# A two-layer diffusion transformer: head outputs summed ungated, the first gate's sums off TensorE, softmax inverses through DRAM, later weight fetches

## The chip, the cores and the metric

The kernel runs on 1 core of one Trainium2 chip. The metric is the device time of one execution in microseconds (us): the median of 3 runs was 1186.27 us before the change (1185.79 to 1186.78). A difference in it under about 2 us is small beside everything that the kernel does: some 5,500 matrix products and 193 MB of transfers.

The engines are named as the profile names them: PE is TensorE's matmul, PEld its weight load, DVE VectorE, ACT ScalarE, POOL GpSimd, and SP the engine that issues most transfers.

## The reference

Two layers over 256 image tokens (x) and 256 context tokens (ctx), D = 1024. Layer 0 mixes tokens by retention (4 heads, values of 512), layer 1 by attention to a neighbourhood of 8 x 16 grid positions plus the context (32 heads of 32). Each layer ends with a squared-relu MLP of 4096. Shift, scale and gate of every part come from a conditioning vector c (c_ctx for the context).

```python
mod = (silu_c @ ada_w[i] + ada_b[i])[:, None, :]
sh1, sc1, g1, sh2, sc2, g2 = jnp.split(mod, 6, axis=-1)
h = x * (1.0 + sc1) + sh1
y, yc = retention_mixer(h, hc, ...)  if i % 2 == 0 else  neighbourhood_mixer(h, hc, ...)
x = layer_norm(DN_ALPHA * x + g1 * y, ln_g[i, 0], ln_b[i, 0])
h = x * (1.0 + sc2) + sh2
x = layer_norm(DN_ALPHA * x + g2 * sq_relu_mlp(h, mlp_w1[i], mlp_w2[i]), ln_g[i, 1], ln_b[i, 1])
# the context goes the same way in layer 0, with its own modulation
# retention:  y = concat over heads( norm(o) * silu(g) ) @ w_o
# neighbourhood:  prob = softmax(concat(q.k + bias, q.k_ctx));  o = prob @ (v, v_ctx)
```

## The kernel before, in words

**Products.** Each f32 product is three products of a high and a low part (`mm3`: hi·hi, hi·lo, lo·hi). A weight unit is a 512 KB block: SP fetches it into one of four `raw` buffers, ACT casts the high part (`hi`), DVE subtracts to get the low part (`lo`). `fetch` issues the transfer and the cast, `lows` the subtraction, `take` hands out units and runs five ahead.

**Order.** A framework puts the instructions of each engine into their final order. Where a line sets `.on` for an engine, its instructions stay in the order written.

**Layer 0.** Eight chunks of 128 columns first (`chunk_*`): each chunk's shift and scale are made on PE, its input is transposed (`chunk_turn`) and modulated, and head 0's Q and V begin. `turn_over` puts filler products on PE ahead of chunk 0. Then come heads 0 to 3. A head has the projections of Q, K and V (Q and V of head 0 fall into the chunks), the rotation on DVE (t, qkh, qkl), gates (pg), scores (pS), the value products (po), and the output projection (pw), each of whose 128x512 results is multiplied by the first gate g1 on DVE (`gated`) and added on POOL to the residual R (`accumulate`). R was scaled by ALPHA on ACT in head 0, so R collects ALPHA·x + g1·y. The last head adds on DVE and is followed by layer norm and the MLP.

**Background stream.** The other modulations are made step by step between the heads' products by `bg()`: each step loads one 512 KB block of `ada_w` and uses the one loaded a step earlier. A part has eight steps. `bg_max` bounds the steps, `bg_until` forces them. The first gate, part (0, 0, 2), runs on PE in head 0 (`ada_mm`: four narrow products a step, into pada); `first_gate` loads it as soon as it is there, since head 0's output needs it. The parts (0, 1, ...) for the MLP of layer 0 are weighted sums on DVE (`weigh`, four 128x512 instructions a step, in spare space named strips). Layer 1's parts are the same in 128x1024 (two instructions a step, acc), and run in layer 0's MLP.

**Layer 1.** The neighbourhood attention takes 16 steps n (8 groups of four heads, two query tiles). The table `STEPS` says for each which weight units are fetched ahead of its scores and softmax (`early`), which behind (`late`), and which projections (K, Q, V) stand between. `scores` writes pqk on PE; `soften` takes the biased minimum on DVE and the exponential with its sum on ACT; `flip` transposes the exponentials (ppt to pt); `attend` multiplies with the values (pav, rows natv) and scales by the inverse sums. For that scaling, `invert` takes the reciprocal of the sums (128x4), DVE spreads it to 128x128 (rr), `flip_sums` transposes it on PE, and `turned` copies it to rt on ACT. V(0) to V(3) are the value projections of the second half of the heads (pnv); the first of them, in the sixth step (n = 5), is the first to use their four weight units.

Of the kernel before, what the change touches and what calls it, by code (L numbers as in the profile page):

```python
# [104 lines left out]
def kernel(  # L105
# [324 lines left out]
    def ada_bias(l, offs, nb):  # L430
        brow = scr("brow")
        ab = ada_b[l]
        for i in range(2):
            sp.dma_start(
                out=brow[64 * i : 64 * i + 64, :nb],
                in_=bass.AP(ab.tensor, ab.offset + offs[i], [[nb, 2], [0, 32], [1, nb]]),
            )
        return brow

    def ada_mm(pr, k, nb, rhs):  # L440

        lhsT = cT[:, k, :, :].rearrange("p a t -> p (a t)")
        for j in range(4):
            pe.matmul(
                pr[32 * j : 32 * j + 32, 0:nb],
                lhsT=lhsT,
                rhs=rhs(j),
                start=(k == 0),
                stop=(k == KC - 1),
                tile_position=(0, 32 * j),  # L450
            )

    def ada_row(pr, brow, nb, p0=0, p1=P, row=None):
        if row is None:
            row = smp.tile([P, 256], F32, tag="row", name=nm("row"), bufs=1)
        dve.tensor_add(out=row[p0:p1, :nb], in0=pr[p0:p1, 0:nb], in1=brow[p0:p1, :nb])
        return row

# [76 lines left out]
    def bg_stream():  # L535
# [3 lines left out]
        for l, w, part in (  # L539
            [(0, 0, 2), (0, 1, 0), (0, 1, 1), (0, 1, 2)]  # L540
            + [(1, 0, 0), (1, 0, 1), (1, 0, 2), (1, 1, 0), (1, 1, 1), (1, 1, 2)]
        ):
            sh, sc, g = 3 * w * D, (3 * w + 1) * D, (3 * w + 2) * D
            offs = (sh + 512 * part, sc + 512 * part) if part < 2 else (g, g + 512)
            for n in range(KC):
                plan.append((l, w, part, offs, n))
        nxt = bg_load(*plan[0])
        yield
        for step, (l, w, part, offs, n) in enumerate(plan):
# [5 lines left out]
            if on_pe(l, w, part):  # L555
                if n == 0:
                    pr = bank("pada")
                if n == KC - 2:
                    brow = ada_bias(l, offs, 256)
                ada_mm(pr, n, 256, lambda j: raw[:, j // 2, (j % 2) * 256 : (j % 2 + 1) * 256])  # L560
                if n == KC - 1:
                    row = ada_row(pr, brow, 256)
                    for t in range(2):
                        pool.dma_start(
                            out=grow[l, w][t].rearrange("(j c) -> j c", j=4), in_=row[t:P:32, :]
                        )
                yield
                continue
            if n == 0:
                red = smp.tile([P, 2, 32], F32, tag="red", name=nm("red"), bufs=2)  # L570
            if l == 0:
# [9 lines left out]
            else:  # L581
                if n == 0:
                    acc = slot(S_VL, [P, 2, D], F32, "acc")
                for t in range(nt):

                    dve.on = n == 0 and (w, part) == (0, 0)
                    weigh(acc[:, t], raw[:].rearrange("p a n -> p (a n)"), t, n, n == 0)
                    dve.on = False
# [14 lines left out]
    bg_max = [39]  # L603
# [341 lines left out]
    chunk_turn(0)  # L945
    chunk_columns(0)
    turn_over(4)
# [73 lines left out]
    def proj_T(th, tl, first=False):  # L1021
        pb = [bank("pq") for _ in range(2)]
        for u in range(2):
            ((wh, wl),) = take(1)
            for dc in range(2):
                for kk in range(4):
                    k = 4 * u + kk
                    mm3(pb[dc][:], (wh[:, kk, tsl(dc)], wl[:, kk, tsl(dc)]), hs(k, 0, NT), k == 0, k == KC - 1)
            if first:
                bg(2)  # L1030
        rotate(pb, th, tl)
# [6 lines left out]
    G1s = [None]  # L1038

    def first_gate():  # L1040

        if G1s[0] is None and bg_done[0] >= 9:
            G1s[0] = load_gate(0, 0, eng=nc.gpsimd)

    for h in range(RH):
        last = h == RH - 1
        if h == 0:
# [6 lines left out]
            act.on = True  # L1054
            for a in range(2):
                act.mul(out=RR[a][:], in_=RR[a][:], mul=ALPHA)
            act.on = False
            proj_T(qkh[:, 2:4], qkl[:, 2:4], True)
        else:
            qkh = slot(S_TH, [P, 4, NT], F32R, "qkh")  # L1060
            qkl = slot(S_TL, [P, 4, NT], F32R, "qkl")
            proj_T(qkh[:, 0:2], qkl[:, 0:2])
            proj_T(qkh[:, 2:4], qkl[:, 2:4])
# [3 lines left out]
            for u in range(4):  # L1067
                ((wh, wl),) = take(1)
                for t in range(4):
                    for kk in range(2):  # L1070
                        k = 2 * u + kk
                        mm3(pv[t][:], hs(k, t * P, (t + 1) * P), (wh[:, kk, :], wl[:, kk, :]), k == 0, k == KC - 1)
                bg()
# [6 lines left out]
        def gates(ts, between=()):  # L1080

            pgs = [bank("pg") for _ in ts]
            for k in range(KC):
# [3 lines left out]
                if h == 0 and k == 3 and len(ts) == 1:  # L1087
                    bg(2)
                    first_gate()
# [39 lines left out]
        if h == 0:  # L1129
# [4 lines left out]
            first_gate()  # L1134
            pg = gate(1)
            act.activation(out=gs[:, 1, :], in_=pg[:], func=AF.Silu)
        else:
            S = masked_scores()
            for t in range(2):
                pg = gate(t)  # L1140
                act.activation(out=gs[:, t, :], in_=pg[:], func=AF.Silu)
                bg()
        ons = []
        for t in range(4):
# [16 lines left out]
            if h == 0 and t == 0:  # L1161
                bg_until(9)
                first_gate()
# [15 lines left out]
        between = {4: lambda: to_oT(0), 5: lambda: to_oT(1)}  # L1179
        for t, pg in zip((2, 3), gates((2, 3), between)):  # L1180
# [3 lines left out]

        bg_until(9)
        first_gate()
        G1 = G1s[0]
# [8 lines left out]
        def tok(t, half, us):  # L1196
            accumulate(tok_mm(t, half, us), t, half, G1)
# [10 lines left out]
        else:  # L1208
            bg_until(39)
            wus = take(4)  # L1210
            wus = (wus[:2], wus[2:])
            gb = slot(S_VL, [P, 2, D], F32, "gb")
            ln_tiles(gb, 0, 0)
# [98 lines left out]
    for hf in range(2):  # L1312
# [9 lines left out]
        if hf == 0:  # L1322
# [33 lines left out]
            hid += hts  # L1356
            outside()
        bg_max[0] = 87
        for fp in range(len(hid), 8):
# [16 lines left out]
        if G2 is None:  # L1376
            G2 = load_gate(0, 1)
        for half in range(2):
# [14 lines left out]
            for u in range(8 - nheld):  # L1393
# [3 lines left out]
                bg()  # L1397
            if not last:
# [244 lines left out]
    def flip(n, sums_too=True):  # L1643
# [11 lines left out]
        if sums_too:  # L1655
            flip_sums(n)

    def flip_sums(n):
        pe.transpose(av_half(n)[:, P:], rrs[n][:].rearrange("p h d -> p (h d)"), ident)
# [4 lines left out]
    def turned(n):  # L1664

        rts[n] = smp.tile([P, P], F32, tag="rt", name=nm("rt"), bufs=2)
# [164 lines left out]
    def W(half, t):  # L1831
# [28 lines left out]
    for n, (early, late, last, before, after) in enumerate(STEPS):  # L1860
        gather(n + 1)
        turned(n)
# [18 lines left out]
    turned(n - 2)  # L1881
    flip(n - 1, False)
# [3 lines left out]
    flip_sums(n - 1)  # L1886
    turned(n - 1)
# [361 lines left out]
```

## Time and profile before

| what | us |
|---|---|
| median of 3 runs | 1186.27 |
| lowest, highest | 1185.79, 1186.78 |
| the profiled execution, its own time | 1188.31 |
| its span, first to last instruction | 1186.5 |
| chunks (0 to 60) | 60.0, PE busy 58.3 |
| head 0 from its K projection (60 to 134.5) | 74.5, PE busy 74.5, DVE 55.3 |
| head 1 (134.5 to 236.2) | 101.7, PE busy 101.7, DVE 76.8 |
| head 2 (236.2 to 337.9) | 101.7, PE busy 101.7, DVE 76.8 |
| last head and its layer norm (337.9 to 441.8) | 103.9, PE busy 103.8, DVE 75.2 |
| MLP of layer 0 (441.8 to 797) | 355.2, PE busy 355.2, DVE 245.7 |
| neighbourhood attention (797 to 987) | 190.0, PE busy 189.5, DVE 133.7 |
| MLP of layer 1 and the end (987 to 1186) | 199.0, PE busy 191.9, DVE 133.9 |

The stages are bounded by the starts of each stage's first products in the chain of waits. A row of the timeline is: start, length, engine, line, operation, output<-inputs, sizes, count; in square brackets stand the idle time before it and what ended it. A row of the chain of waits is: start, length, engine and what it wrote, count of instructions. All instructions carry line 84, since one helper issues them all; they are told apart by the names of their tiles.

### The profile page before, as it was taken

Reading aid. Unit: us, or ns where it says so; the run is one execution under the profiler, and the core shown is the slowest. Engines: PE = TensorE matmul, PEld = TensorE weight load, DVE = VectorE, ACT = ScalarE, POOL = GpSimd, SP = SyncE. Lnnn points to the kernel's source line nnn. Section 1 sums busy time; section 2 is a strip of 40 time slices with the busy share of each in tenths; the row PEclk is TensorE's granted clock in tenths of the full one; section 3 lists DMA queues with packets and bytes.
Section 4 is the critical chain, followed back from the end, with each engine's and each line's share of the span. In section 5 each row is a group of like instructions: output and inputs, shape, how many; then the busy total and the mean of one; then the engine's idle time right before and its main releaser. Section 6 shows DMA issues by size and latency. Waiting matters only on the chain.

```text
span 1186.5 us, 17867 instructions
## 1 busy us (share of the span) xinstructions
PE 1176.7 (99%) x6884; PEld 990.9 (84%) x6884; DVE 832.8 (70%) x1304; ACT 480.9 (41%) x813; POOL 248.9 (21%) x389
## 2 busy tenths in 40 slices
PE   9999999999999999999999999999999999999997
PEld 7778888888888889888888888889888878999886
DVE  3876975886688487757876675668467588876446
ACT  3652222322223246441212333137466666665341
POOL 0104301310330141780202000223344430000001
PEclk9999999999999999999999999999999999999999
DMA  9964441444254216756566665637244434765660
GB/s 276 273 234 161 142 158 56 143 130 137 89 160 160 77 55 209 203 112 215 177 193 211 200 213 185 206 108 215 69 143 125 118 122 152 224 201 185 227 212 36
DMA packets 138041, 193.16 MB, mean 163 GB/s; under 512 B 9772, under 2 KB 81108, under 8 KB 137956
## 3 DMA queue, kind: packets, MB, share of 16 engines
q1 hardware_dynamic: 129572, 179.02, 47.3%
q0 software_dynamic: 7232, 10.44, 3.9%
q10 hardware_dynamic: 1152, 2.56, 0.7%
q8 instruction: 54, 0.88, 0.3%
q14 instruction: 31, 0.25, 0.1%
HBM read 187.15 MB, written 5.75 MB: 163 GB/s over the span
## 4 chain that ended last, share of the span: by engine, by line
PE 96%; ACT 1%; DVE 1%; issue 1%; DMA 0%; POOL 0%; DVEq 0%; ACTq 0%
PE p L84 44%; PE pq L84 8%; PE pg L84 7%; PE pv L84 7%; PE pw L84 7%; PE pn L84 5%; PE pnv L84 4%; PE po L84 3%; PE pada L84 2%; PE pnw L84 1%; PE pS L84 1%; PE ppt L84 1%; PE pqk L84 1%; PE pt L84 1%; PE pav L84 1%; PE p1t L84 1%
## 5 line engine op out<-in xcount | busy, mean ns | idle before, releaser
L84 ACT CAST hi<-raw 128x1024 fp32r<-128x1024 f32 (+2 forms) x228 | 232.7, 1032 | 325.0 <-PE p L84 151.3
L84 DVE TENSOR_TENSOR lo<-raw,hi 128x1024 fp32r<-128x1024 f32 (+2 forms) x228 | 280.3, 1240 | 101.8 <-ACT hi L84 101.0
L84 PE MATMUL p<-hi,hid 128*128 128x512 f32 (+1 forms) x832 | 241.8, 374 | 0.0
L84 PEld LDWEIGHTS p<-hi,hid 128*128 128x128 f32 x832 | 152.1, 188 | 27.7
L84 PE MATMUL p<-hTh,lo 128*128 128x256 f32 (+1 forms) x512 | 166.9, 329 | 0.0
L84 PE MATMUL p<-hTl,hi 128*128 128x256 f32 (+1 forms) x512 | 166.9, 329 | 0.0
L84 PE MATMUL p<-hTh,hi 128*128 128x256 f32 (+1 forms) x512 | 164.0, 330 | 0.0
L84 PE MATMUL p<-lo,hid 128*128 128x512 f32 (+1 forms) x416 | 155.3, 373 | 0.0
L84 DVE SCALAR_TENSOR_TENSOR acc<-rawa,scol,acc 128x1024 f32<-128x1024 f32 x56 | 74.7, 1344 | 63.1 <-DMA rawa<-in_ada_w_dram 62.9
L84 POOL TENSOR_TENSOR R<-R,acc 128x512 f32<-128x512 f32 x40 | 62.2, 1565 | 212.3 <-DVE acc L84 212.2
L84 PEld LDWEIGHTS p<-hTl,hi 128*128 128x128 f32 x512 | 96.4, 188 | 8.7
L84 PEld LDWEIGHTS p<-hTh,lo 128*128 128x128 f32 x512 | 96.3, 188 | 8.8
L84 PEld LDWEIGHTS p<-hTh,hi 128*128 128x128 f32 x512 | 95.1, 190 | 8.7
L84 PEld LDWEIGHTS p<-lo,hid 128*128 128x128 f32 x416 | 78.4, 188 | 13.6
L84 ACT CAST hid<-r 128x256 fp32r<-128x256 f32 (+1 forms) x64 | 31.9, 500 | 103.4 <-DVE r L84 103.3
L84 DVE SCALAR_TENSOR_TENSOR strips<-rawa,scol,strips 128x512 f32<-128x512 f32 x84 | 66.4, 847 | 0.0
L84 POOL TENSOR_TENSOR rstd<-rstd,misc 128x1 f32<-128x1 f32 x28 | 19.2, 686 | 215.5 <-DVE rstd L84 214.3
L84 ACT ACTIVATE s<-s,mn 128x512 f32<-128x512 f32 x64 | 45.5, 712 | 26.2 <-DVE mn L84 26.1
L84 PE MATMUL pg<-hi,hTh 128*128 128x512 f32 x128 | 51.1, 399 | 0.0
L84 PE MATMUL pw<-hi,oh 128*128 128x512 f32 x128 | 50.9, 398 | 0.0
L84 PE MATMUL pg<-lo,hTh 128*128 128x512 f32 x128 | 50.0, 391 | 0.0
L84 PE MATMUL pw<-hi,ol 128*128 128x512 f32 x128 | 50.0, 390 | 0.0
(238 smaller groups left out, 2277.1 us busy)
## 6 DMA issues: line engine op xcount, KB each, us to landing
raw<-in_mlp_w_dram SPq DMA_DIRECT2D x128, 512.0 KB, 4.2
rawa<-in_ada_w_dram SPq DMA_DIRECT2D x80, 512.0 KB, 4.3
raw<-in_ret_w_in_dram SPq DMA_DIRECT2D x42, 512.0 KB, 3.6
raw<-in_nat_w_in_dram SPq DMA_DIRECT2D x24, 512.0 KB, 3.9
rawq<-in_ada_w_dram SPq DMA_DIRECT2D x16, 512.0 KB, 5.8
raw<-in_ret_w_o_dram SPq DMA_DIRECT2D x16, 512.0 KB, 4.4
bias<-rpb_rows POOLq DMA_DIRECT2D x32, 128.0 KB, 2.9
raw<-in_nat_w_o_dram SPq DMA_DIRECT2D x8, 512.0 KB, 4.1
```

The costliest lines, as they stand in the source:

```text
L84: r = f(*args, **kwargs)
```

## The change

It makes seven edits.

1. The first gate is no product on PE any more (`ada_mm`, `ada_bias`, `ada_row`, `on_pe` go). `EARLY` names the parts that run as 128x512 sums on DVE in the heads: (0,0,2), (0,1,0) and (0,1,1). Part (0,1,2), the gate of layer 0's MLP, moves into that MLP, as 128x1024 sums.
2. The heads' outputs are summed without the gate: head 0 copies them into R on ACT, heads 1 and 2 add on DVE. In the last head `residual_in` fetches x and ctx again (8 transfers of 256 KB), multiplies the sum by g1 and adds ALPHA·x: 16 DVE instructions of 128x512. The last head's own output is gated as before. R is no longer scaled on ACT. The gate is loaded by SP at the start of head 2.
3. The layer norm's rows (`gb`) of layer 0's MLP are loaded later, into the gate's space.
4. The second to sixth rows of `STEPS` (n = 1 to 5) fetch nothing ahead of the scores and softmax any more: their one or two units, in the sixth row the first of two, are fetched behind.
5. The inverses of steps 0 to 14 go through DRAM: POOL writes the 128x4 reciprocals turned, SP reads them back spread over the rows of rt. Step 15 keeps the old way.
6. In chunk 0 the modulation's columns come between two pairs of transposes, with one filler product fewer.
7. `bg_max` for the heads falls from 39 to 31, and the MLP's first half makes eight more background steps.

```diff
-    def on_pe(l, w, part):
-        return (l, w, part) == (0, 0, 2)
+    EARLY = (0, 0, 2), (0, 1, 0), (0, 1, 1)
...
     def bg_load(l, w, part, offs, n):
-        if l == 1 or w == 0:
+        if (l, w, part) not in EARLY:
             return ada_load(l, n, offs)
...
-            if on_pe(l, w, part):
-                if n == 0:
-                    pr = bank("pada")
...
-                ada_mm(pr, n, 256, lambda j: raw[:, j // 2, (j % 2) * 256 : (j % 2 + 1) * 256])
...
-            if l == 0:
+            if (l, w, part) in EARLY:
                 dve.on = True
...
-    bg_max = [39]
+    bg_max = [31]
...
-    def chunk_turn(k):
-        pts[k] = bank("pt")[:, 0:256], prs[k][:, 256:512]
-        for t in range(4):
+    def chunk_turn(k, ts=range(4)):
+        if k not in pts:
+            pts[k] = bank("pt")[:, 0:256], (prs[k][:, 256:512] if k else bank("pt")[:, 0:256])
+        for t in ts:
             pe.transpose(pts[k][t // 2][:, tsl(t % 2)], R[t][:, tsl(k)], ident)
...
-    chunk_turn(0)
+    chunk_turn(0, (0, 1))
     chunk_columns(0)
-    turn_over(4)
+    chunk_turn(0, (2, 3))
+    turn_over(3)
...
+    def residual_in(t):
+        for half in range(2):
+            sl = slice(half * 512, (half + 1) * 512)
+            xin = scr("xin")
+            sp.dma_start(out=xin[:], in_=(x, ctx_in)[t // 2][0][tsl(t % 2), sl])
+            dve.tensor_mul(out=R[t][:, sl], in0=R[t][:, sl], in1=G1[:, t // 2, sl])
+            dve.scalar_tensor_tensor(
+                out=R[t][:, sl], in0=xin[:], scalar=ALPHA, in1=R[t][:, sl], op0=ALU.mult, op1=ALU.add
+            )
...
-            for a in range(2):
-                act.mul(out=RR[a][:], in_=RR[a][:], mul=ALPHA)
...
+            if h == 2:
+                G1 = load_gate(0, 0, eng=nc.sync)
+            if last:
+                residual_in(0)
             proj_T(qkh[:, 0:2], qkl[:, 0:2])
+            if last:
+                residual_in(1)
...
+        if last:
+            between[1] = lambda: residual_in(3)
...
         def tok(t, half, us):
-            accumulate(tok_mm(t, half, us), t, half, G1)
+            ps = tok_mm(t, half, us)
+            o = R[t][:, half * 512 : (half + 1) * 512]
+            if h == 0:
+                act.copy(out=o, in_=ps[:])
+            else:
+                dve.tensor_add(out=o, in0=ps[:], in1=o)
...
+            gb = cpool.tile([P, 2, D], F32, tag="G", name=nm("gb"))
+            ln_tiles(gb, 0, 0)
...
             if hf:
                 bg(2 + fp % 2)
+            else:
+                bg(2 if fp > 5 else 1)
...
+    inverses = dram.tile([NS, 4, P], F32, tag="inverses", name="inverses")
     def invert(n):
-        rr = rrs[n] = smp.tile([P, 4, HD], F32, tag="rr", name=nm("rr"), bufs=1)
         dve.reciprocal(out=sums[n][:], in_=sums[n][:])
-        dve.tensor_copy(out=rr[:], in_=sums[n][:].unsqueeze(2).broadcast_to([P, 4, HD]))
+        if n < NS - 1:
+            row = inverses[n]
+            pool.dma_start(out=row.rearrange("j q -> q j"), in_=sums[n][:])
+            rts[n] = smp.tile([P, P], F32, tag="rt", name=nm("rt"), bufs=3)
+            sp.dma_start(
+                out=rts[n][:], in_=bass.AP(row.tensor, row.offset, [[P, 4], [0, HD], [1, P]])
+            )
+            return
+        rrs[n] = scr("rr")[:, :P].rearrange("p (j d) -> p j d", j=4)
+        dve.tensor_copy(out=rrs[n], in_=sums[n][:].unsqueeze(2).broadcast_to([P, 4, HD]))
...
-        if sums_too:
+        if n == NS - 1:
             flip_sums(n)
...
         (1, 0, 0, [K(2)], []),
-        (2, 0, 0, [K(3)], []),
-        (2, 0, 0, [K(4)], []),
-        (1, 0, 0, [K(5)], []),
-        (2, 0, 0, [Q(2)], []),
-        (1, 1, 0, [V(0)], []),
+        (0, 2, 0, [K(3)], []),
+        (0, 2, 0, [K(4)], []),
+        (0, 1, 0, [K(5)], []),
+        (0, 2, 0, [Q(2)], []),
+        (0, 2, 0, [V(0)], []),
```

The order of the instructions moves at three places that matter below. On PE, in head 0 between the first gate's products (pg) and the scores (pS; hTl and hTh are the input's low and high parts), before:

```order
L84 MATMUL pg_900<-hi_835,hTl 128x512
L84 MATMUL pg_900<-hi_835,hTh 128x512
L84 MATMUL pada_828<-rawa_913,cT 32x256 x4
L84 MATMUL pg_900<-lo_836,hTh 128x512
L84 MATMUL pg_900<-hi_835,hTl 128x512
L84 MATMUL pS_940<-qkh_760 128x256
L84 MATMUL pS_940<-qkl_761,qkh_760 128x256
```

and with the change:

```order
L84 MATMUL pg_877<-hi_824,hTl 128x512
L84 MATMUL pg_877<-hi_824,hTh 128x512
L84 MATMUL pg_877<-lo_825,hTh 128x512
L84 MATMUL pg_877<-hi_824,hTl 128x512
L84 MATMUL pS_905<-qkh_760 128x256
L84 MATMUL pS_905<-qkl_761,qkh_760 128x256
```

The four narrow products for the gate (pada) are gone, and the scores follow the gate's products directly; the second score product still reads qkl.

On ACT, in the sixth step of the neighbourhood attention (hi casts a weight unit, s is the softmax's exponential, R receives the value projection V(0)), before:

```order
L84 CAST oTh_6957<-rt_7687 128x4x32
L84 COPY rt_7834<-pav_6956 128x128
L84 CAST hi_7838<-raw_7836 128x1024
L84 ACTIVATE s_7860,sums_7859<-s_7860,mn_7858 128x512
L84 ACTIVATE s_7863,sums_7859<-s_7863,mn_7858 128x512
L84 ACTIVATE s_7866,sums_7859<-s_7866,mn_7858 128x512
L84 ACTIVATE s_7869,sums_7859<-s_7869,mn_7858 128x512
L84 CAST hi_7874<-raw_7872 128x1024
L84 COPY R_105<-pnv_7878 128x512
```

and with the change:

```order
L84 CAST oTh_6928<-rt_7509 128x4x32
L84 ACTIVATE s_7814,sums_7813<-s_7814,mn_7812 128x512
L84 ACTIVATE s_7817,sums_7813<-s_7817,mn_7812 128x512
L84 ACTIVATE s_7820,sums_7813<-s_7820,mn_7812 128x512
L84 ACTIVATE s_7823,sums_7813<-s_7823,mn_7812 128x512
L84 CAST hi_7828<-raw_7826 128x1024
L84 CAST hi_7833<-raw_7831 128x1024
L84 COPY R_105<-pnv_7838 128x512
```

The copy of the inverses to rt is gone, and the first of the two casts (hi_7828, which the last quarter of V(0) reads) now stands behind the four exponentials.

On SP, at the end of the neighbourhood attention (raw is a weight unit of the output projection, rt an inverse read back, gb two layer-norm rows), before:

```order
L84 DMA raw_8844<-in_nat_w_o_dram 128x2x512
L84 DMA raw_8961<-in_nat_w_o_dram 128x2x512
L84 DMA raw_8998<-in_nat_w_o_dram 128x2x512
L84 DMA gb_8966<-lns 128x1024 x2
L84 DMA raw_9019<-in_mlp_w_dram 128x4x256
```

and with the change:

```order
L84 DMA raw_8788<-in_nat_w_o_dram 128x2x512
L84 DMA rt_8419<-inverses 128x1x128
L84 DMA rt_8521<-inverses 128x1x128
L84 DMA raw_8902<-in_nat_w_o_dram 128x2x512
L84 DMA rt_8636<-inverses 128x1x128
L84 DMA raw_8939<-in_nat_w_o_dram 128x2x512
L84 DMA rt_8743<-inverses 128x1x128
L84 DMA gb_8907<-lns 128x1024 x2
L84 DMA raw_8960<-in_mlp_w_dram 128x4x256
```

Four reads of inverses, each of which waits for its write, now stand among the last weight units; rt_8743 is the one of step 14.

More of the change, by code (lines that the diff above doesn't have):

```diff
@@ L428, in ada_load @@
         return raw
[L430 to L457, printed above, removed]
     def folded(red, acc, t, c0, n):
@@ L584, in bg_stream @@
                 for t in range(nt):
-                    dve.on = n == 0 and (w, part) == (0, 0)
+                    dve.on = n == 0 and l == 0
                     weigh(acc[:, t], raw[:].rearrange("p a n -> p (a n)"), t, n, n == 0)
@@ L1053 @@
             evac_v(pv, vh, vl)
-            act.on = True
-            for a in range(2):
-                act.mul(out=RR[a][:], in_=RR[a][:], mul=ALPHA)
-            act.on = False
-            proj_T(qkh[:, 2:4], qkl[:, 2:4], True)
+            proj_T(qkh[:, 2:4], qkl[:, 2:4])
         else:
@@ L1072 @@
                         mm3(pv[t][:], hs(k, t * P, (t + 1) * P), (wh[:, kk, :], wl[:, kk, :]), k == 0, k == KC - 1)
+                if last and u == 1:
+                    residual_in(2)
                 bg()
@@ L1397 @@
                 bg()
+                if G2 is None and u == 3:
+                    G2 = load_gate(0, 1)
             if not last:
@@ L1861 @@
         gather(n + 1)
-        turned(n)
         fetch(early)
@@ L1880 @@
     gather(n - 1)
-    turned(n - 2)
-    flip(n - 1, False)
+    flip(n - 1)
     fetch(1)
```

48 lines of the change are left out of this document (9 added, 39 removed).

## The prediction, made before the changed kernel was run

> **What bounds the kernel now.** I read the page's totals first, then its chain of waits, then TensorE's starts by time.
>
> ```profile
> span 1186.5 us, 17867 instructions
> PE 1176.7 (99%) x6884; PEld 990.9 (84%) x6884; DVE 832.8 (70%) x1304; ACT 480.9 (41%) x813; POOL 248.9 (21%) x389
> PE 96%; ACT 1%; DVE 1%; issue 1%; DMA 0%; POOL 0%; DVEq 0%; ACTq 0%
> ```
>
> The chain runs through PE for 96% of the span, at a granted clock of 1.00 in the windows quoted below. So an edit pays if it takes matmuls away or closes a gap between them, and everything else is worth what it makes PE wait. Busy time can't show a gap of a few hundred ns, since matmuls overlap; I count by starts and by stretches of the chain. A fully fed run of 96 matmuls takes 21.76 us there, 0.227 each.
>
> **The gate off PE.** Head 0 carries first-gate products on PE (pada, two steps per piece of 1.00 us); head 1 does the same work without them.
>
> ```profile
> 60.14 5.50 PE pq L84 x24
> ...
> 71.88 1.00 PE pada L84 x16
> ...
> 87.86 1.00 PE pada L84 x16
> ...
> 134.54 21.76 PE pq L84 x96
> ...
> 178.06 4.18 PE pS L84 x24
> ...
> 236.24 21.76 PE pq L84 x96
> L84 PE MATMUL pada<-rawa,cT 128*32 128x256 f32 x64 | 4.7, 388 | 0.0
> L84 DVE SCALAR_TENSOR_TENSOR strips<-rawa,scol,strips 128x512 f32<-128x512 f32 x84 | 66.4, 847 | 0.0
> ```
>
> From its K projection to its end, head 0 took 134.54 − 60.14 = 74.40 us. Head 1 took 236.24 − 178.06 = 58.18 from its scores, and its K projection is half of 21.76, 10.88: together 69.06. The change turns the first into the second: **−5.34** (the x64 records alone are 4.7 busy). Head 1's stretch holds one folding matmul, so the one that the DVE way adds is in it. DVE takes the gate's eight steps over, but the third feed-forward part leaves the heads, so the 84 weighted sums at 0.85 us stay 84 there.
>
> **The scores of head 0.** With pada gone, PE comes to the scores sooner than DVE has what they read.
>
> ```profile
> 76.20 0.41 DVE L84 TENSOR_TENSOR t<-t 128x256 f32<-128x256 f32 x1
> 77.56 1.05 ACT L84 CAST hi<-raw 128x1024 fp32r<-128x1024 f32 x1 [2.96 <-DMA raw<-in_ret_w_o_dram]
> 78.64 1.22 DVE L84 TENSOR_TENSOR lo<-raw,hi 128x1024 fp32r<-128x1024 f32 x1 [2.03 <-ACT hi L84]
> 79.79 0.42 DVE L84 TENSOR_TENSOR qkl<-t,qkh 128x256 fp32r<-128x256 f32 x1
> ```
>
> PE: 60.14 + 10.88 + half a gate (5.44) = 76.46. DVE, in its printed order: the last rotation ends 76.61, the weight's lo 1.22, the last qkl 0.42: 78.25. The lo's present wait of 2.03 for a late weight goes, as that fetch no longer stands behind four gate loads on SP. The first products don't need this qkl, which covers 0.4: **+1.4**. If the weight stays as late as now, PE waits until 80.21, 3.7; if DVE is ahead, 0.
>
> **Matmuls in the neighbourhood layer.** Fifteen transposes of inverses leave PE.
>
> ```profile
> L84 PE MATMUL pav<-cst,rr 128*128 128x128 f32 x16 | 4.5, 280 | 0.0
> 914.48 0.27 PE L84 MATMUL pav<-cst,rr 128*128 128x128 f32 x1
> 914.59 0.39 PE L84 MATMUL pav<-pt,G 128*128 128x128 f32 x2
> ```
>
> By starts one costs 914.59 − 914.48 = 0.11: 15 × 0.11 = **−1.7**.
>
> The Trainium skill (Trainium Kernel Development and Optimization, Performance Expectations) calls a matmul's duration in a profile a bad measure because matmuls are pipelined. The trace agrees: by mean duration (0.28) the fifteen would be 4.2 and the time 2.5 less.
>
> **Chunk 0.**
>
> ```profile
> 9.01 0.44 PE L84 MATMUL pada<-cst,R 128*128 128x128 f32 x2
> 9.28 0.51 PE L84 MATMUL pada<-cst,row 128*128 128x2 f32 x4
> ```
>
> The columns go ahead of two transposes (9.28 − 9.01 = 0.27 sooner), and one filler matmul goes: **−0.2**, between 0 (the next weights aren't there sooner) and −0.4.
>
> **The moved fetches.** Each step's scores (pqk) wait for a DVE and ACT whose lows and casts stand before the softmax; a clean one takes 0.90.
>
> ```profile
> 875.99 0.49 PE L84 MATMUL pqk<-kT,qT 32*128 32x512 f32 x2
> 876.82 1.31 PE pqk L84 x9
> 878.13 5.71 PE pn L84 x24
> ...
> 886.39 1.28 PE pqk L84 x12
> ...
> 896.16 1.64 PE pqk L84 x11
> ...
> 906.02 1.53 PE pqk L84 x11
> ...
> 915.77 0.90 PE pqk L84 x9
> 916.67 5.67 PE pnv L84 x24
> 920.29 0.19 ACT L84 ACTIVATION_READ_ACCUMULATOR s<-s,mn 128x1 f32 x1
> ```
>
> Over 0.90 stand 878.13 − 875.99 − 0.90 = 1.24, then 0.38, 0.74 and 0.63: 3.0 to win. Behind the softmax casts come late instead. In the sixth step the last quarter of V(0) is cast after the exponentials: in the clean step they end at 920.48, so hi 921.53 (1.05) and lo 922.75 (1.22). PE reaches that quarter after 18 of 24 products, 916.67 + 4.25 = 920.92, and its lo one product later, 921.15: 1.6 late, 2.0 with some lag from the step ahead. The third and fifth steps, which cast two units late, I give 0.3 each, a little less than the smallest excess of now (0.38). Net −3.0 + 2.6 = **−0.4**; −3.0 if no cast is late, +1 if both two-unit steps lag like the sixth.
>
> **The inverses by DMA.** Their round trip replaces DVE's copy, PE's transpose and ACT's copy, and the trace doesn't show it. The deadline that matters is the last (n = 14).
>
> ```profile
> 972.05 0.18 DVE L84 RECIPROCAL sums<-sums 128x4 f32<-128x4 f32 x1
> 979.66 0.29 DVE L84 TENSOR_TENSOR rt<-pav,rt 128x128 f32<-128x128 f32 x1
> 980.73 0.23 DVE L84 COPY rr<-sums 128x128 f32<-128x128 f32 x1
> 981.01 0.33 PE L84 MATMUL pav<-cst,rr 128*128 128x128 f32 x1
> L84 POOL DMA_DIRECT2D rpb_rows<-rpb_neg x79 | 46.3, 596 | 9.9 <-DMA rpb_rows<-far 8.0 <-DMA rpb_rows<-rpb_neg 1.0 <-issue 0.8
> rpb_rows<-rpb_neg POOLq DMA_DIRECT2D x49, 14.0 KB, 3.3
> gb<-lns SPq DMA_DIRECT2D x6, 512.0 KB, 4.7
> rows<-in_ada_b_dram SPq DMA_DIRECT2D x3, 8.0 KB, 2.8
> ```
>
> Slack: 979.66 − 972.23 = 7.4. POOL's issue is 0.60, its small writes land in 3.3, SP's reads in 2.8 to 4.7: 6.7 to 8.6. DVE's multiply waits; behind it stand oTl, the last reciprocal, and the copy to rr that PE takes 0.05 after it ends, so any excess reaches PE. I take **+0.5**, between 0 and 2.8 (a write slower by 1.6). The read also stands on SP ahead of two LN rows and the MLP's first weights. Their buffers come free later than that, and I charge nothing.
>
> The Trainium skill (DMA: Bandwidth & Descriptors, Anatomy of one DMA — SWDGE (gpsimd) path) puts some 2.0 us of fixed cost on one DMA; two would be about 4, inside the slack, an estimate that makes this term 0 and the time 0.5 less. The trace's 2.8 to 4.7 is longer.
>
> **Work that I cost at nothing.**
>
> ```profile
> 337.90:441.80 103.90, 103.84 (x481) 85.72 (x480) 75.16 (x127) 34.01 (x53) 22.29 (x26) 1.00 0.34 108
> 441.80:797.00 355.20, 355.20 (x1700) 296.90 (x1699) 245.70 (x290) 115.73 (x164) 81.43 (x111) 1.00 0.60 186
> L84 DVE SCALAR_TENSOR_TENSOR acc<-rawa,scol,acc 128x1024 f32<-128x1024 f32 x56 | 74.7, 1344 | 63.1 <-DMA rawa<-in_ada_w_dram 62.9
> ```
>
> The ungated sums swap one DVE instruction for another and relieve POOL; ACT, which makes the copies in head 0, is busy 41% of the span. The last head gains 16 DVE operations of about 0.7 and one more weighing step (4 × 0.85): 75.2 + 14.6 = 89.8 of 103.9 us. That is tight: **+0.3**, 0 to 3. The eight steps moved into the MLP are 16 × 1.34 = 21.5 us of DVE in a window where it has 109 free: 0. If that cover were gone, up to 21.5 would show.
>
> **Sum:** −5.3 + 1.4 − 1.7 − 0.2 − 0.4 + 0.5 + 0.3 = −5.4, so a span of 1181.1. The profiled execution took 1188.31 with its start and end; the runs' median, 1186.27, is 2.0 under that and 0.2 under the span. So **1180.8**. Of the bounds, half of those of the scores, the fetches and the tail on either side give 1178.5 to 1183.5. A measurement here can't tell less than 0.2% (2.4 us) from no change: faster means under 1183.9, slower over 1188.6.
>
> **Rivals.**
>
> A, PE takes all of it. DVE is idle 2.03 before that lo now, and the casts after the exponentials may find ACT ahead. Then the scores, the sixth step, the tail and the last head cost nothing: −5.3 − 1.7 − 0.2 − 2.4 = −9.6, **1176.7**. Against it: the 1.64 us of arithmetic on DVE that I count in full.
>
> B, the bound passes to DVE where PE shrinks. Head 0 waits 3.7, the last head 3, and the NAT steps come to +1: the sum is −5.3 + 3.7 − 1.7 − 0.2 + 1 + 0.5 + 3 = +1.0; midway between that and my sum, −2.2, gives **1184.1**, no change that can be told. For it: 89.8 of 103.9 in the last head. Against it: nothing on DVE there is due at once.
>
> C, slower, by the inverses alone: the write scatters 512 single four-byte elements (128x4 turned). The round trip W is hidden up to 7.4; beyond, all later work moves by W − 7.4. The other edits give −5.9 without the tail's 0.5, so from W = 15.7 it decides for slower (2.4 + 5.9 + 7.4). At W = 18, the tail costs 10.6: **1190.9**. For it: no row has such small pieces. Against it: writes of rpb_rows land in 3.3.
>
> The Trainium skill (DMA: Bandwidth & Descriptors, Rules for kernel authors) warns of just this: a transpose by a plain DMA with a rearranged pattern makes a descriptor per element and is many times slower. No row here has one, so it lifts C's chance only a little.
>
> **Chances.** My forecast 0.50, A 0.23, B 0.15, C 0.08, anything else 0.04. Faster are the forecast, A, and a little of the rest: 0.75. Same is 0.16, mostly B; slower 0.09, mostly C. The range that leaves out about 2 in 10 runs from 1176.2, below A's own value, to 1185.5, over B's.
>
> **What would show it.** Head 0 from its K projection to head 1's start: 70.5 us (69.1 under A, over 72 under B). A wait of 1.4 for qkl before pS there. Scores of NAT steps near 0.90, and a gap near 2 before the last quarter of V(0). The reciprocal to the read's landing for n = 14 near 8 us: 5 or less speaks for A, over 15 for C. I am wrong altogether if PE's starts show gaps over 1 us in the last head or the MLP.

## The result: 1.3% slower, and the profile after

The changed kernel takes 1202.88 us (median of 4 runs, 1199.88 to 1204.98) against 1186.53 before (median of 4, the three above and one more): a ratio of 1.0134, 95% interval 1.0122 to 1.0146. The forecast was 1180.8 us, faster. The profiled execution spans 1203.2 us, 16.7 more than the one before. First its page (the last row is POOL's transfer queue: packets, MB, share of the transfer engines' time):

```profile
span 1203.2 us, 17752 instructions
PE 1174.1 (98%) x6806; PEld 989.0 (82%) x6806; DVE 838.1 (70%) x1316; ACT 478.1 (40%) x804; POOL 226.1 (19%) x379
PE 71%; DVE 11%; DMA 11%; issue 4%; ACT 2%; POOL 1%; DVEq 0%; ACTq 0%; POOLq 0%
q0 software_dynamic: 7456, 9.42, 6.8%
```

and the borders of the stages in its chain of waits (start, length, engine and tile, count):

```profile
59.82 10.94 PE pq L84 x48
70.76 5.44 PE pg L84 x24
76.20 4.20 PE pS L84 x24
...
128.54 21.76 PE pq L84 x96
...
435.70 2.88 PE p L84 x24
...
794.71 2.87 PE pn L84 x24
```

PE's busy time fell by 2.6 us as work left it, and yet its share of the chain fell from 96% to 71%: PE now waits, for DVE and for transfers. The borders, laid beside those of before (441.76 and 797.23), say where:

| stretch | before | after | difference |
|---|---|---|---|
| chunks, to 60.14 | 60.14 | 59.82 | −0.32 |
| head 0 from its K projection | 74.40 | 68.72 | −5.68 |
| heads 1 to 3 | 307.22 | 307.16 | −0.06 |
| MLP of layer 0 | 355.47 | 359.01 | +3.54 |
| neighbourhood attention to the end | 389.27 | 408.49 | +19.22 |

The first three parts bring 6.1 us, a little more than rival A gave for them. The last row loses three times that, and it holds more than the attention. Behind the attention stands layer 1's MLP, of which the change edits nothing. The last 1104 products in its chain, before the change:

```profile
1016.92 162.12 PE p L84 x1104
```

and with it:

```profile
1034.58 159.35 PE p L84 x1104
```

PE waits in neither, and the granted clock is 1.00 in both; in that execution of the kernel before, the 128x256 products simply start 0.118 us apart and not 0.113. The traces don't tell why. The end behind these products takes 9.27 us and not 7.46. Taken up to the first of the 1104 products, the attention costs 219.69 us before and 239.87 after, so it loses 20.2 us. Its pieces in the chain, then the transfers' median time from issue to landing (last number of a row), of the changed kernel:

```profile
866.27 8.99 DMA inverses<-sums
...
879.17 10.26 DMA bias<-rpb_rows
...
893.34 6.20 DMA bias<-rpb_rows
...
970.54 6.91 DMA bias<-rpb_rows
...
986.66 5.93 DMA rt<-inverses
```

```profile
bias<-rpb_rows POOLq DMA_DIRECT2D x32, 128.0 KB, 5.5
...
bias<-rpb_rows POOLq DMA_DIRECT2D x32, 96.0 KB, 7.8
...
inverses<-sums POOLq DMA_DIRECT2D x15, 2.0 KB, 11.7
```

and the bias rows of the kernel before:

```profile
bias<-rpb_rows POOLq DMA_DIRECT2D x32, 128.0 KB, 2.9
...
bias<-rpb_rows POOLq DMA_DIRECT2D x32, 96.0 KB, 2.5
```

Two things stand out. A write of 2 KB lands after 11.7 us. And the chain has more bias rows in it than inverses (17.5% against 9.3% of its time between 840 and 1000 us): the softmax's bias, which the change does not touch, comes two to three times as late, and DVE's biased minimum, the exponential and all that follow wait for it. TensorE's waits in the timeline of the changed kernel show what stood behind:

```profile
577.18 0.26 PE L84 MATMUL pada<-red,cst 128*32 128x16 f32 x8 [1.99 <-DVE acc L84]
...
903.58 0.80 PE L84 MATMUL pnv<-hi,hTh 128*128 128x512 f32 x1 [5.42 <-ACT hi L84]
```

The longest names a cast, hi for the last quarter of V(0), which the change moved behind the exponentials. The other row stands in layer 0's MLP, where the prediction named a gap of over 1 us as a sign of being wrong altogether. The page alone leaves two readings: that the moved cast is the fault, or that it only stands behind exponentials that wait for bias.

### The profile page after: what moved, and what is told of

The parts are those of the page before. It is cut to its first block, busy times and chain, and to the rows that moved or that the text cites. A ratio compares the mean times of both kernels' runs of the same rounds, so it can differ in the third digit from the quotient of the medians.

```text
span 1203.2 us, 17752 instructions
## 1 busy us (share of the span) xinstructions
PE 1174.1 (98%) x6806; PEld 989.0 (82%) x6806; DVE 838.1 (70%) x1316; ACT 478.1 (40%) x804; POOL 226.1 (19%) x379
## 3 DMA queue, kind: packets, MB, share of 16 engines
q0 software_dynamic: 7456, 9.42, 6.8%
## 4 chain that ended last, share of the span: by engine, by line
PE 71%; DVE 11%; DMA 11%; issue 4%; ACT 2%; POOL 1%; DVEq 0%; ACTq 0%; POOLq 0%
PE p L84 24%; PE pq L84 8%; PE pv L84 7%; PE pw L84 7%; PE pg L84 7%; DMA rawa<-in_ada_w_dram 6%; DVE acc L84 4%; PE pnv L84 4%; DVE lo L84 3%; PE pn L84 3%; PE po L84 3%; DMA bias<-rpb_rows 2%; PE pS L84 1%; PE pada L84 1%; PE ppt L84 1%
## 5 line engine op out<-in xcount | busy, mean ns | idle before, releaser
L84 DVE TENSOR_TENSOR lo<-raw,hi 128x1024 fp32r<-128x1024 f32 (+2 forms) x228 | 273.6, 1215 | 103.6 <-ACT hi L84 102.8
L84 DVE SCALAR_TENSOR_TENSOR acc<-rawa,scol,acc 128x1024 f32<-128x1024 f32 x70 | 92.9, 1336 | 67.3 <-DMA rawa<-in_ada_w_dram 67.3
L84 POOL TENSOR_TENSOR rstd<-rstd,misc 128x1 f32<-128x1 f32 x28 | 19.2, 687 | 214.3 <-DVE rstd L84 213.1
L84 POOL TENSOR_SCALAR rstd<-mv 128x1 f32<-128x1 f32 x16 | 3.9, 244 | 290.0 <-DVE mv L84 290.0
L84 DVE SCALAR_TENSOR_TENSOR strips<-rawa,scol,strips 128x512 f32<-128x512 f32 x84 | 57.6, 747 | 0.0
L84 POOL TENSOR_TENSOR R<-R,acc 128x512 f32<-128x512 f32 x16 | 25.9, 1633 | 165.6 <-DVE acc L84 165.5
L84 PE MATMUL pg<-hi,hTl 128*128 128x512 f32 x128 | 49.9, 390 | 0.0
```

The costliest lines, as they stand in the source:

```text
L84: r = f(*args, **kwargs)
```

## The experiments

Times are medians. Each ratio is to runs of the kernel before in the same session, whose medians lay between 1186.53 and 1188.44. "MLP from", "MLP" and "attention to the end" are the stages of the table above, and "to the 1104" is the attention up to the first of layer 1's last 1104 products, in the one profiled execution of each. The kernel before, e10 and e11 took 162.12 us for these products and the others 159.33 to 159.35, so "to the 1104" is the column to compare.

| kernel | us | ratio to before, interval | MLP from | MLP | attention to the end | to the 1104 |
|---|---|---|---|---|---|---|
| before | 1186.53 | | 441.76 | 355.47 | 389.27 | 219.69 |
| after | 1202.88 | 1.0134 (1.0122 to 1.0146) | 435.70 | 359.01 | 408.49 | 239.87 |
| e1 inverses on PE | 1186.24 | 0.9991 (0.9975 to 1.0007) | 436.13 | 355.92 | 389.45 | 222.57 |
| e2 fetches early | 1212.90 | 1.0211 (1.0196 to 1.0227) | 436.43 | 359.06 | 415.31 | 246.64 |
| e3 write from SP | 1232.05 | 1.0377 (1.0355 to 1.0398) | 435.99 | 360.79 | 436.92 | 269.90 |
| e4 write unturned | 1183.80 | 0.9976 (0.9950 to 1.0001) | 435.69 | 362.28 | 385.83 | 218.03 |
| e5 second gate in heads | 1185.80 | 0.9987 (0.9969 to 1.0005) | 438.03 | 355.46 | 389.31 | 222.48 |
| e6 sixth step early | 1183.80 | 0.9956 (0.9935 to 0.9977) | 436.24 | 359.33 | 385.33 | 218.54 |
| e7 all mended | 1180.98 | 0.9942 (0.9926 to 0.9959) | 439.09 | 356.28 | 385.13 | 218.25 |
| e8 one inverse by DRAM | 1199.56 | 1.0092 (1.0071 to 1.0112) | 435.97 | 361.85 | 397.58 | 230.33 |
| e9 gate steps spread | 1181.10 | 0.9955 (0.9938 to 0.9973) | 437.72 | 355.46 | 385.22 | 218.33 |
| e10 writes unread | 1204.33 | 1.0140 (1.0110 to 1.0171) | 436.06 | 361.38 | 409.36 | 237.92 |
| e11 gate done before last head | 1186.62 | 0.9987 (0.9976 to 0.9998) | 442.55 | 358.70 | 388.15 | 218.44 |
| e12 PE inverses, fetches early | 1185.98 | 0.9991 (0.9971 to 1.0011) | 436.11 | 356.52 | 386.57 | 219.74 |

**e1, the inverses back on PE**

```diff
-        if n < NS - 1:
-            row = inverses[n]
-            pool.dma_start(out=row.rearrange("j q -> q j"), in_=sums[n][:])
...
+        dve.tensor_copy(out=rr[:], in_=sums[n][:].unsqueeze(2).broadcast_to([P, 4, HD]))
```

> All inverses are turned by PE again, as before the change (fifteen transposes, DVE's spread and ACT's copy are back); everything else is the changed kernel's. Theory D: the 19.2 us that the changed kernel loses from the start of the neighbourhood attention on come from the inverses' way through DRAM. Then that stretch falls to 389 us or a little below, the wait of 5.4 us ahead of V(0)'s last quarter falls to about 2, the granted clock there is 1.00, and the time is 1182 to 1184.5. Rival F: the fetches behind the softmax lose it, as the longest wait (5.4 us, for the cast of V(0)'s last quarter) stands on them. Then the time stays at 1197 or above.

Theory D. Up to the 1104 products the attention falls from 239.87 to 222.57 us, with the fetches still behind the softmax: 17.3 of the 20.2 us come from the inverses' way through DRAM. The other 2.9 come with the moved fetches (e6, e12): at V(0) PE still waits 1.67 and 0.76 us, and the clock behind that is 0.50, not 1.00 as expected. The time came out above the range expected. The profiled execution, 1183.47, lies within that range, so what the slower ones lose stays open; the MLP's loss below is a candidate.

**e2, the fetches back ahead of the softmax, inverses by DRAM**

```diff
-        (0, 2, 0, [V(0)], []),
+        (1, 1, 0, [V(0)], []),
```

and the four rows above it in the same way.

> The fetch rows of the second to sixth steps are back ahead of the softmax; the inverses still go through DRAM. Theory D: bias rows arrive late whatever the fetches do; the time stays within 5 us of 1202.9, with waits elsewhere in the steps. Rival F: the loss goes, 1182 to 1187.

F falls: nothing is won back. The kernel is even slower, by 10 us where D allowed 5, with bias rows landing in 8.4 to 9.0 us. Why casts ahead of the late softmax make it worse wasn't tried.

**e3, the write from SP**

```diff
-            pool.dma_start(out=row.rearrange("j q -> q j"), in_=sums[n][:])
+            sp.dma_start(out=row.rearrange("j q -> q j"), in_=sums[n][:])
```

> The writes of the inverses are issued by SP on its own queue and not by POOL; the 512 four-byte pieces stay. Theory Q: what costs is that the write stands among the bias loads, on POOL's stream and queue (bias rows land in 5.5 to 7.8 us there, 2.5 to 2.9 before). Then bias lands in about 3 us again and the time falls to 1183 to 1189. Rival L: what costs is the round trip itself, about 18 us from the reciprocal to rt. Then the time stays above 1195.

Theory Q as put here falls. Off POOL's queue the writes take as long, and the bias rows, now alone on that queue, are as late:

```profile
bias<-rpb_rows POOLq DMA_DIRECT2D x32, 128.0 KB, 5.9
...
bias<-rpb_rows POOLq DMA_DIRECT2D x32, 96.0 KB, 8.0
...
inverses<-sums SPq DMA_DIRECT2D x15, 2.0 KB, 11.8
```

So it isn't the place in POOL's stream that holds the bias up. Nor do the rows merely wait in a queue, for the queue's packets themselves take longer. POOL's queue moves as many in e1 as here, with no write of inverses among them; first its row in e1, then in e3:

```profile
q0 software_dynamic: 6976, 9.39, 3.8%
```

```profile
q0 software_dynamic: 6976, 9.39, 7.1%
```

Nor is L shown by this, as the bias is late whoever writes. The attention is 28 us longer than in the changed kernel; SP also fetches the weights and now waits for each reciprocal, but what of the 28 that makes wasn't tried.

**e4, the write unturned: 128 pieces of 16 bytes**

```diff
-            pool.dma_start(out=row.rearrange("j q -> q j"), in_=sums[n][:])
+            pool.dma_start(out=bass.AP(row.tensor, row.offset, [[4, P], [1, 4]]), in_=sums[n][:])
```

> POOL writes the 128x4 reciprocals as they lie, 128 pieces of 16 bytes, so the turn is left out and the attention is scaled by wrong inverses; queue, order and the read are unchanged. Theory P: the 512 four-byte pieces are what is slow. Then the write lands in 3 to 6 us (11.7 with the pieces) and the time falls to 1183 to 1190. Rival Q2: any further transfer on POOL's queue does it. Then the time stays above 1195.

Theory P. One line makes 19 us by the medians. On its page and among its transfers:

```profile
q0 software_dynamic: 7456, 9.42, 3.9%
...
bias<-rpb_rows POOLq DMA_DIRECT2D x32, 128.0 KB, 3.0
...
inverses<-sums POOLq DMA_DIRECT2D x15, 2.0 KB, 2.6
```

POOL's queue moves the same 7456 packets and 9.42 MB as in the changed kernel, in 3.9% of the transfer engines' time and not 6.8%; the write lands in 2.6 us and not 11.7; the bias is as prompt as before. The turned write differs from this one in the number, the size and the addresses of its pieces; which of the three counts, the run doesn't tell. Up to the 1104 products the attention takes 218.03 us, 4.5 below e1; about 2 of these are e1's longer wait and slow clock at V(0), and the rest is what inverses by DRAM would bring if they came without the pieces.

**e8, one inverse through DRAM, that of step 14**

```diff
+        if n == NS - 2:
+            row = inverses[n]
+            pool.dma_start(out=row.rearrange("j q -> q j"), in_=sums[n][:])
...
```

> As the first run of this study, but the inverse of step 14 alone goes through DRAM, with its 512 four-byte pieces. Theory W: one round trip is long by itself, 15 to 18 us against a slack of 7.4, as in the rival of the prediction; it costs 6 to 10 us at the end of the attention. Theory Z: the loss comes from fifteen writes that hold up the bias rows and each other; one write, with no bias row left to fetch behind it, is back in 8 to 10 us and costs 0 to 3.

Theory W, at 7.8 us over e1 up to the 1104 products. Its chain of waits:

```profile
974.37 9.06 DMA inverses<-sums
983.49 4.87 DMA rt<-inverses
```

DVE's timeline, with the reciprocal and the multiply that waits for it:

```profile
973.84 0.18 DVE L84 RECIPROCAL sums<-sums 128x4 f32<-128x4 f32 x1
...
988.45 0.29 DVE L84 TENSOR_TENSOR rt<-pav,rt 128x128 f32<-128x128 f32 x1 [6.92 <-DMA rt<-inverses]
```

and windows, in which the granted TensorE clock is the third figure from the end:

```profile
985.50:989.80 4.30, 0.00 (x0) 0.00 (x0) 0.95 (x5) 1.02 (x3) 0.00 (x0) 0.50 0.89 290
989.80:995.60 5.80, 5.80 (x35) 4.42 (x36) 3.14 (x6) 1.68 (x5) 0.00 (x0) 0.50 0.50 158
995.70:1005.00 9.30, 9.30 (x54) 8.09 (x53) 8.40 (x15) 4.21 (x6) 0.57 (x1) 1.00 0.37 113
```

The reciprocal ended at 974.02; the read landed 14.3 us later, at 988.36, a little less than W's 15 to 18, and the multiply waited 6.92, near 14.3 − 7.4. Behind it the products run at a clock of 0.50 up to 995.6, of which more below.

**e10, the writes made, and never read**

```diff
         dve.tensor_copy(out=rr[:], in_=sums[n][:].unsqueeze(2).broadcast_to([P, 4, HD]))
+        if n < NS - 1:
+            pool.dma_start(out=inverses[n].rearrange("j q -> q j"), in_=sums[n][:])
```

> As the first run of this study (inverses turned by PE and used), and POOL writes the reciprocals, turned, to DRAM as in the changed kernel, which nothing reads. Nobody waits for a round trip here. Theory Q: the four-byte pieces hold up the bias rows; those land in 5 us or more, and the time is 1192 to 1202. Theory L: the loss in the changed kernel is the wait for the round trips alone, 14.4 us (as the one of step 14 by itself took) against their slack; then bias rows land in 3 us and the time is 1182 to 1188.

This is the decisive run. PE turns the inverses and no engine reads what was written, and yet the attention takes 237.92 us up to the 1104 products, near the changed kernel's 239.87: the unread writes alone bring back 15.4 of the 17.3 us. Theory Q in this form holds: the pieces hold up the bias. The time, 1204.33, came out above the range that Q gave. This run's profile has no landing times for POOL's transfers, but in its chain between 840 and 1000 us single waits for bias<-rpb_rows reach 14.83 us. The head line of that chain (G<-rpb_rows is bias as well, the part that is kept in G's space):

```profile
by line: DMA bias<-rpb_rows 26.4%; DMA G<-rpb_rows 16.7%; PE pnv L84 10.5%; issue 9.0%; PE ppt L84 7.3%; POOL bias L84 4.3%; PE pav L84 4.3%; PE pn L84 3.6%; PE pnw L84 2.8%; PE pqk L84 2.5%; DVE s L84 2.5%; DVE lo L84 1.8%; ACT s L84 1.8%; 
```

**e6 and e12, the fetches with inverses on PE**: e6 is e1 with one early fetch in the sixth step, e12 with all rows as before the change.

> As the first run of this study, but the sixth step fetches one of its two units ahead of the softmax again. Theory S: that cast, late behind the exponentials, is the 2.9 us at V(0)'s last quarter. Then the neighbourhood attention to the end takes 386.5 to 387 us instead of 389.5. Rival T: the wait moves to that step's scores, 389 us.

> As the first run of this study (inverses on PE), with the fetch rows of the second to sixth steps back ahead of the softmax. It is the move of the fetches alone, undone. By the prediction's term (3.0 saved at the scores, 2.6 lost behind), the attention to the end takes 390 us instead of 389.6. If the move is worth what the scores waited, it takes 392 or more; if the cast of V(0)'s last quarter with what follows costs more than the scores saved, 388 or less.

S, and more than was expected: 218.54 us up to the 1104 products against 222.57. In e1 TensorE stood idle there for casts behind the exponentials:

```profile
895.41 0.39 PE L84 MATMUL pnv<-hi,hTl 128*128 128x512 f32 x1
897.47 0.50 PE L84 MATMUL pnv<-hi,hTh 128*128 128x512 f32 x1 [1.67 <-ACT hi L84]
898.73 0.50 PE L84 MATMUL pnv<-lo,hTh 128*128 128x512 f32 x1 [0.76 <-DVE lo L84]
```

By starts that is 2.06 − 0.23 and 1.26 − 0.23, together 2.9 us; the clock of 0.50 behind them costs some 1.6 more (last section). e12 gives 219.74, the kernel before's 219.69 again: the move as made costs 2.8 us, and without the sixth step it saves 1.2. The medians don't show the 2.8: e1 and e12 have the same ratio, and their runs spread over 8 and 11 us.

**e5, e7, e9, e11, the second gate's sums back in the heads** (e5 on e1's base, the others on e6's):

```diff
-    EARLY = (0, 0, 2), (0, 1, 0), (0, 1, 1)
+    EARLY = (0, 0, 2), (0, 1, 0), (0, 1, 1), (0, 1, 2)
...
-    bg_max = [31]
+    bg_max = [41]
...
-            else:
-                bg(2 if fp > 5 else 1)
```

with the ten more steps in head 0 and in the output projection of head 1 (e5, e7); in the value projections of heads 1 and 2 (e9); and two of them at the end of head 2, the gate's row asked for at once (e11).

> As the first run of this study (inverses on PE), and the MLP gate's sums (part (0,1,2)) stand in the heads again, as 128x512 sums on DVE with the gate's: ten more background steps in heads 0 to 2, none more in the MLP. Theory M: the eight steps in the MLP's first half take the lead of the weight fetches there, so DVE waits for blocks of modulation weights and PE behind DVE (the wait of 2.2 us at the end of the first half's products in the changed kernel, 3.8 in the run with unturned writes), by an amount that differs from run to run. Then the MLP of layer 0 takes 355.5 us, the runs lie within 2 us of each other, and the time is 1181 to 1183. Rival H: the loss there comes from the later load of the layer norm's rows, or the heads pay for the ten steps. Then the MLP's wait stays, or heads 1 and 2 take over 102.5 us, and the time is 1185 or more.

> The two edits above together: inverses on PE, the second gate in the heads, one early fetch in the sixth step. Theories M and S: 1178 to 1180.5, with runs within 2 us. If M is wrong, 1182 or above; if S is wrong, 1181 to 1183.

> As the seventh run of this study, but the ten steps of the second gate stand in the value projections of heads 1 and 2 and no more in head 1's output projection, so that its last step falls into the last head's value projection. Theory G: what the heads paid there (1.4 us in head 1, where DVE's sums stood ahead of the output's; 1.9 us in the last head, where DVE waited for the gate's bias row just before the layer norm) was the place of the steps. Then the MLP begins at 436 us and the time is 1177 to 1179. Rival: DVE is too full in the heads wherever they stand; then it begins at 438.5 or later and the time stays at 1180 to 1182.

> As the ninth run of this study, with two more of the ten steps in head 2's output projection, so that the second gate's sums end with head 2 and its bias row is asked for at the start of the last head. Theory G: the 1.75 us ahead of the last head's layer norm (DVE waited 1.7 us for that bias row there, with the last sums behind it) goes; the MLP begins at 436 to 436.5 and the time is 1178 to 1180. Rival: the sums at the end of head 2 hold up the first weights of the last head, and the MLP begins at 437.5 or later.

The MLP takes 355.46, 356.28 and 355.46 us in e5, e7 and e9, as before the change; the nine kernels that keep the steps in it take 355.92 to 362.28, in single executions. e11 speaks against a simple account: its steps stand in the heads too, and its MLP takes 358.70, with 2.6 us of PE waiting for weights (lo). So the MLP loses up to 7 us with the steps in it and can lose 3 without them; that the steps are the cause is likely and not shown. e5's runs spread as widely (1184.56 to 1192.98) as e1's (1182.21 to 1189.94): M's claim about the spread fell, and its time, 1185.80, is in rival H's range. The heads pay 1.6 to 3 us in return (MLP from 437.7 to 439.1 and not 436.1), so e5 wins nothing by itself. e9's place of the steps saved 1.4 of that, not the 3 expected: the last head still waits for the gate's bias row.

```profile
416.95 0.21 DVE L84 TENSOR_TENSOR gate<-gate 32x64 f32<-32x64 f32 x1 [1.67 <-DMA gate<-in_ada_b_dram]
```

e11 made it worse, as its rival said: the sums at the end of head 2 held the last head's first products up by 3.5 us. e7, e9 and e6 beat the kernel before, by 0.6%, 0.5% and 0.4%; e7 came out 0.5 us above the times expected, e9 2.1 us.

## Why the prediction was wrong

The step that failed is the inverses by DMA, "I take +0.5, between 0 and 2.8". It measured +17.3 us (the changed kernel against e1, up to the 1104 products; 16.6 by the medians).

- **The price came from the wrong rows.** The writes of rpb_rows (3.3) and reads (2.8 to 4.7) that bounded the round trip move neighbouring elements together, the 14 KB write of rpb_rows in pieces of 64 bytes. The write here moves 512 single elements of four bytes. It took 9.06 us as the only one of its kind (e8) and 11.7 in the changed kernel; with pieces of 16 bytes it took 2.6 (e4), and no multiply waited for an inverse there, as the step had it. The "bounds" were bounds of another kind of transfer.
- **The place was too narrow.** I looked for the deadline of the last inverse alone. Its excess is real: 6.9 us in e8. In the changed kernel five of the fifteen multiplies waited for their inverse, 19.2 us in all on DVE, the one of n = 13 the longest, with 20.9 us from its reciprocal to its read's landing. But e10 loses 15.4 us without a single reader. What the fifteen writes take from the bias rows is enough for most of the loss, and it wasn't in the sum. DVE's multiply for n = 13 in the changed kernel:

```profile
992.69 0.29 DVE L84 TENSOR_TENSOR rt<-pav,rt 128x128 f32<-128x128 f32 x1 [6.32 <-DMA rt<-inverses]
```

- **Rival C** named the 512 pieces as its mechanism and was given 0.08. Its price at W = 18, 1190.9, was a latency past a slack; for n = 14 W was 14.3 in e8 and at most 14.6 in the changed kernel, under its own threshold of 15.7, and the kernel was slower all the same. So C had the right pieces and the wrong path. The sentence of the Trainium skill beside it (DMA: Bandwidth & Descriptors, Rules for kernel authors), on transposing by a rearranged pattern, warned of the right thing; "it lifts C's chance only a little" was the misjudgement. By e4 against the changed kernel the pieces make a factor of 4.5 in the write's landing.
- **The moved fetches**, −0.4, measured +2.8 (e1 against e12). The mechanism was right, the place too: the wait at the last quarter of V(0) was put at 2.0 and is 2.9. It left out the clock, which was 0.50 for 3.4 us after it. And the scores brought less than the 3.0: in e1 the scores of two steps still took 1.58 and 1.53 us, so some 1.7 were won.
- **The MLP's eight steps**, 0, measured +3.5 in the profiled execution and 0.5 to 6.8 in those of the other kernels that have them. DVE had the room that was counted. In the changed kernel's trace DVE waits 2.29 us for a late block of modulation weights at 574.10, and the sums that PE waits for at 577.18 (1.99 us) stand behind it in order. That moving the steps made the block late isn't shown (e11).

What held, and one term that did not:

- **The gate off PE** and **the scores of head 0**: −5.34 + 1.4 foretold, −5.68 measured; the first held, the 1.4 did not come. PE reaches the scores at 76.20, as worked out (76.46), DVE finishes the last qkl at 77.89 (78.25 foretold), and PE still doesn't wait: its 24 score products run 4.20 us from their start without a gap, so 1.7 us of them can't need that qkl, where I had counted 0.4. That is rival A's value for this term. DVE's timeline of the changed kernel:

```profile
76.33 1.22 DVE L84 TENSOR_TENSOR lo<-raw,hi 128x1024 fp32r<-128x1024 f32 x1
77.47 0.42 DVE L84 TENSOR_TENSOR qkl<-t,qkh 128x256 fp32r<-128x256 f32 x1
```

- **Chunk 0**: −0.2 foretold, −0.32 measured. That can't be told from nothing: with the same chunks, e4's end at 59.79 us and e2's at 60.62. **The last head**: +0.3 foretold; heads 1 to 3 together changed by −0.06.
- **The fifteen transposes** were put at −1.7. No run takes them out alone; e4, without them and with prompt transfers, is 4.5 below e1 up to the 1104 products, about 2 of it at V(0).

Without its inverses, the change would have been level with the kernel before by the medians (e1, ratio 0.9991). Of its 6 us in head 0 and the chunks, the moved fetches give back 2.8; where the rest goes in the executions slower than the profiled one isn't shown.

## What to carry to other kernels

Price a transfer by its pieces as well as its bytes: here 2 KB landed in 2.6 us as 128 pieces and in 9 to 12 us as 512. A row of the trace is a bound only for transfers with such pieces, and one without such a row deserves a wide range upward. A slow transfer's cost isn't only its own latency; list what else is in flight in that stage with a deadline (here the bias rows), and ask what that costs if it comes at half speed. And where several edits go in together, the ones that gain and the ones that lose sit in different stages: compare the stages before the totals, and cut off stretches that no edit touches, since they can differ between two executions (here by 2.8 us in the last MLP).

## What the hardware showed that was not expected

- The four-byte writes slow transfers on other queues: with the writes on SP's queue the bias rows on POOL's land in 5.9 and 8.0 us (e3), 2.9 and 2.5 without them, and the packets of POOL's queue take 7.1% of the transfer engines' time and not 3.8%. Through which part they hold each other up, the runs don't tell.
- The granted TensorE clock can fall to 0.50 behind a wait of some 2 us, and then stays there for 3.4 us (e1), 6.8 (the changed kernel, from 903.1) or 10.2 (e8). In e1 it was 0.50 from 899.2 to 902.6 after the waits at V(0), and the products' starts were 0.43 apart and not 0.23; in e8 it was 0.50 from 985.5 to 995.6, around a wait of 6.6. It need not fall: the same two waits at V(0) in e8 (1.69 and 0.77 us) and the one of 1.99 us in the changed kernel's MLP left it at 1.00. From the product after the second wait to that step's last transpose PE took 4.19 us in e1 and 2.57 in e8, so the fall cost e1 some 1.6 us beyond the waits. Before the change no wait of PE behind the chunks was longer than 0.34 us and the clock of these stages was 1.00. The Trainium skill (TensorE: Matmul & The Clock Gate, Part 1: The HAM clock gate) has the clock halve after an idle window of about 3.4 us; in e1 waits of 1.67 and 0.76 us, one product apart, were enough.

```profile
880.00:895.00 15.00, 14.81 (x128) 12.48 (x126) 11.91 (x32) 8.48 (x23) 4.54 (x12) 1.00 0.54 154
899.20:902.50 3.30, 3.30 (x14) 2.80 (x13) 0.92 (x2) 1.06 (x2) 0.83 (x2) 0.50 0.89 214
902.70:915.00 12.30, 12.30 (x123) 9.73 (x122) 6.83 (x21) 5.79 (x16) 3.17 (x8) 1.00 0.27 78
```

These are windows of e1; the 0.50 and 1.00 are the granted clock.
